# The rows of h without gaps, at another address, in a two-layer decoder trunk on one core

## The chip, the core and the metric

The kernel runs on one NeuronCore of a Trainium2 chip. Its engines are PE (TensorE, matmuls; its weight loads are listed as PEld), DVE (VectorE), ACT (ScalarE), POOL (GpSimd) and SP (SyncE, which here issues DMAs). The core's memory SBUF has 128 partitions; a tile takes the same bytes in each of them, so "address" below means the byte within a partition. The metric is the device time in microseconds of one execution. Three runs of the kernel before took 2653.11, 2655.77 and 2656.17 us, median 2655.77.

## The reference

Two layers over 256 tokens of width 2048, all in float32. Layer 0 mixes tokens by an eight-head retention, layer 1 by a short gated convolution; each is followed by a SwiGLU feed-forward with an inner width of 5632. Every sub-layer does

```python
mod = (c_act @ w_mod[i] + b_mod[i])[:, None, :]
sh1, sc1, g1, sh2, sc2, g2 = jnp.split(mod, 6, axis=-1)
h = (rms_norm(x, norm1_g[i]) * (1.0 + sc1) + sh1).astype(x.dtype)
y = retention_mixer(h, ...)            # or short_conv_mixer
x = (x + g1 * y).astype(x.dtype)
h = (rms_norm(x, norm2_g[i]) * (1.0 + sc2) + sh2).astype(x.dtype)
x = (x + g2 * swiglu(h, ffn_w_in[i], ffn_w_out[i])).astype(x.dtype)
```

and a final RMSNorm closes the trunk. Nearly all the arithmetic is products of h, or of a result of such a product, with weight matrices that are read once from HBM.

## The kernel before

Activations stand transposed: 128 features on the partitions, the 256 tokens along the row. A matrix of 2048 features is 16 such row tiles. Each float32 value is split into two parts that a matmul takes at its fast float32 format, hi (the rounded value) and lo (what is left); an activation row holds 256 hi columns and then 256 lo columns. A weight block of 128x128 is split alike: raw weights come by DMA (`fetch`, L289, three buffers), ACT casts half of a raw tile to hi (L310) and DVE subtracts for lo (L313), two halves ahead of their use (`AHEAD`).

The order on PE is written out by the program; weights lie in HBM in exactly that order (`in_use_order`), so `take` (L318) hands out the blocks one after another. A product of activations with weights takes one of these forms:

- `product` (L345): for each row k and each column block, a **pair**: one matmul of hi against the row's 512 columns (L355) and one of lo against its 256 hi columns (L358). It is the form of both feed-forward inputs and of the convolution's input, which read h, and of all output projections, which read `mid` (feed-forward and convolution) or `rm` (retention).
- `packed` (L365): three matmuls of 256 columns (L378 to L380). It reads h in the retention's input, and mid or rm in the last block of an output.
- `values` (L794): h is the weight side and 512 columns of hi or lo stream past it (L801 to L803).
- `normed` (L470): the first column blocks of a feed-forward or convolution input, before the norm of x is known. `scaled_only` (L461) writes rows that lack the norm, `ends` (L479, L480) writes two more columns behind each half row with the shift, and three matmuls of 258 columns run on each row (L493 to L495). Meanwhile `modulated` (L453) makes the finished rows with the norm in them, in the same memory, for the column blocks that follow.

All engines but PE are ordered by a scheduling layer, which places an instruction as soon as what it reads is written and what it overwrites has been read.

h is one tile of 16 rows, `[P, KT, 2, S + 2]` floats, so a row takes 2 x 258 x 4 = 2064 bytes, of which the four columns of `ends` are a gap for the finished rows. In the built program the tile begins at byte 118496, which is 1760 modulo 2048; row j thus begins at 1760 + 16j modulo 2048. The tiles of mid and rm are 2048 bytes each and follow each other without a gap; all begin at 2016 modulo 2048. Weight tiles hi and lo begin at 1760 modulo 2048.

The input of the first feed-forward has 44 column blocks in its first part, of which `normed` takes 6, and 44 in its second; the convolution's has 48, of which `normed` takes 6. With 16 rows each this makes stretches of 608, 704, 672, 608 and 704 pairs on h (3296 in all), with the outputs' stretches on mid between them.

Of the kernel before, what the change touches and what calls it, by code (L numbers as in the profile page):

```python
# [10 lines left out]
F32 = mybir.dt.float32  # L11
F32R = mybir.dt.float32r
I32 = mybir.dt.int32
AF = mybir.ActivationFunctionType
ALU = mybir.AluOpType
PSUM = bass.MemoryType.PSUM

P = 128
D = 2048
S = 256  # L20
KT = D // P
# [27 lines left out]
STEPS = (8, 8, 24, 12)  # L49
RAW_BUFS = 3  # L50
PART_BUFS = 4

Q0, K0, V0, G0 = 0, HEADS * DK, 2 * HEADS * DK, 2 * HEADS * DK + HEADS * DV
SH1, SC1, GT1, SH2, SC2, GT2 = range(6)
# [131 lines left out]
def trunk(ctx: ExitStack, tc: tile.TileContext, x_in, c_in, pos_in, w_mod, cols_in, tab_in, w_all, out):  # L186
    nc = tc.nc
    const = ctx.enter_context(tc.tile_pool(name="const", bufs=1))
    work = ctx.enter_context(tc.tile_pool(name="work", bufs=2))
    wpool = ctx.enter_context(tc.tile_pool(name="wpool", bufs=PART_BUFS))  # L190
    ps = ctx.enter_context(tc.tile_pool(name="ps", bufs=8, space=PSUM))
# [7 lines left out]
    def tmp(tag, shape=(P, S), dtype=F32, pool=work, bufs=None):  # L199
        return pool.tile(list(shape), dtype, tag=tag, name=name(tag), bufs=bufs)  # L200
# [8 lines left out]
    x = [t[:, j, :] for t in x4 for j in range(4)]  # L209
# [57 lines left out]
    def paced(n):  # L267

        units[0] += n
        due = 0  # L270
        for (a, i), (b, j) in zip(plan_mod, plan_mod[1:]):
            if units[0] >= a:
                due = min(j, i + (units[0] - a) * (j - i) // (b - a))
        allowed[0] = min(allowed[0] + n * MOST, 2.0) if n <= 64 else 0.0
        while todo and n_mod - len(todo) < due and allowed[0] >= 1.0:
            allowed[0] -= 1.0
            modulation(*todo.pop())

    def needed(layer, which, last=KT - 1):
        while any(m[:2] == (layer, which) and m[2] <= last for m in todo):  # L280
            modulation(*todo.pop())
# [36 lines left out]
    def take(group, k, col):  # L318

        assert order.pop() == (group, k, col)  # L320
        i = taken_cols[0] % HALF
        if i == 0:
            if ready and taken_cols[0]:
                ready.pop(0)
            while len(ready) < 1 + AHEAD * (units[0] >= first):
                n = len(ready)
                prepare()
                if len(ready) == n:
                    break
        taken_cols[0] += group.width  # L330
        return [t[:, i : i + group.width] for t in ready[0]]

    def bank():
        return ps.tile([P, 2, S], F32, tag="bank", name=name("bank"))
# [73 lines left out]
    def norm_sums(accs):  # L408

        pt = bank()  # L410
        for i, acc in enumerate(accs):
            for t in range(2):
                nc.tensor.matmul(
                    pt[:, 0, t : t + 1], acc[:, t * P : (t + 1) * P], ones[:, 0:1],
                    start=i + t == 0, stop=i == len(accs) - 1, skip_group_check=True,
                )
        return pt

    def norm_roots(pt, n):

        r = tmp("rs", (P, 2), bufs=4)
        nc.vector.tensor_scalar(r, pt[:, 0, 0:2], 1.0 / n, EPS, op0=ALU.mult, op1=ALU.add)
        r2 = tmp("rs", (P, 2), bufs=4)
        nc.gpsimd.tensor_tensor(r2, r, half, op=ALU.pow)
        return r2

    def norm_spread(r):

        pb = bank()
        for t in range(2):  # L430
            nc.tensor.matmul(
                pb[:, 0, t * P : (t + 1) * P], r[:, t : t + 1].to_broadcast([P, P]), ident, start=True, stop=True
            )
        return pb[:, 0, :]
# [18 lines left out]
    def modulated(h, j, rb, layer, norm):  # L453
        shifted(h, scaled(j, rb, layer, norm), j, layer, norm)

    hpool = ctx.enter_context(tc.tile_pool(name="hpool", bufs=1))

    h_all = hpool.tile([P, KT, 2, S + 2], F32R, tag="h", name="h")
    h = [h_all[:, j, :, :S] for j in range(KT)]

    def scaled_only(layer, norm, j):  # L461

        needed(layer, SC2 if norm else SC1, j)
        a = mod_a[layer][norm][:, j : j + 1]
        nc.scalar.activation(h[j][:, 0, :], x[j], AF.Identity, scale=a)
        nc.vector.scalar_tensor_tensor(
            h[j][:, 1, :], x[j], a, h[j][:, 0, :].bitcast(F32), op0=ALU.mult, op1=ALU.subtract
        )

    def normed(accs, layer, norm, g):  # L470

        needed(layer, SH2 if norm else SH1)
        shift = mod_s[layer][norm].unsqueeze(2).to_broadcast([P, KT, 2])
        ends = [h_all[:, :, i, S:] for i in range(2)]
        nc.scalar.copy(ends[0], shift)  # L479
        nc.vector.tensor_tensor(ends[1], shift, ends[0].bitcast(F32), op=ALU.subtract)  # L480
        banks = [bank().rearrange("p a b -> p (a b)")[:, : S + 2] for _ in g.cols]
        made = [0]

        def more(n):
            while made[0] < n:
                modulated(h[made[0]], made[0], root, layer, norm)
                made[0] += 1

        for k in g.ks:
            rows = [h_all[:, k, i, :] for i in range(2)]  # L490
            for c, pt in zip(g.cols, banks):
                hi, lo = take(g, k, c)
                nc.tensor.matmul(pt, hi, rows[0], start=k == 0, stop=False)  # L493
                nc.tensor.matmul(pt, hi, rows[1], start=False, stop=False)  # L494
                nc.tensor.matmul(pt, lo, rows[0], start=False, stop=k == KT - 1)  # L495
            if k == ROOTS_AT:
                r = norm_roots(norm_sums(accs), D)
            elif k == SPREAD_AT:
                root = tmp("rb", bufs=1)
                nc.scalar.copy(root, norm_spread(r))  # L500
            elif k > SPREAD_AT:
                more(min(k, made[0] + 2))
        more(KT)
        paced(len(g.cols) * len(g.ks))

        def total(pt, dst=None):
            end = tmp("end", (P, 1), bufs=2)
            nc.scalar.copy(end, pt[:, S : S + 1])
            t = tmp("low", bufs=3)
            nc.vector.tensor_tensor(t, pt[:, :S], root, op=ALU.mult)  # L510
            dst = tmp("sum", bufs=4) if dst is None else dst
            nc.scalar.activation(dst, t, AF.Identity, bias=end)
            return dst

        return [lambda dst=None, pt=pt: total(pt, dst) for pt in banks]
# [27 lines left out]
    with ExitStack() as inner:  # L543
# [353 lines left out]
        def ret_out(part, last):  # L897
            after = (lambda j: scaled_only(0, 1, j)) if last else None
            acc = output(RET_OUT[part], mid, (0, GT1), last, after, base=0)
            assert not asides  # L900
            for n in range(len(mid)):
                if ("mid", n) in tag_of:
                    free.append(tag_of.pop(("mid", n)))
            return acc
# [13 lines left out]
    def swiglu(layer, acc, after):  # L918
        n = FT // 2
        for part, groups in enumerate(FFN_IN):  # L920
            mid = [mpool.tile([P, 2, S], F32R, tag=f"mid{i}", name=name("mid")) for i in range(n)]
            pending, done = [], 0
            for i, g in enumerate(groups):
                pending += [sums(g)] if part or i else normed(acc, layer, 1, g)
                while len(pending) >= 2:
                    a, b = pending[:2]
                    pending = pending[2:]
                    s = a()
                    g1 = tmp("silu", pool=mpool, bufs=2)
                    nc.scalar.activation(g1, s, AF.Silu)  # L930
                    s = b()
                    m = tmp("m", pool=mpool, bufs=2)
                    nc.vector.tensor_tensor(m, s, g1, op=ALU.mult)
                    split(mid[done], m)
                    done += 1
            acc = output(FFN_OUT[part], mid, (layer, GT2), part == 1, after if part else None)
        return acc

    acc = swiglu(0, acc, lambda j: scaled_only(1, 0, j))


    mid = [mpool.tile([P, 2, S], F32R, tag=f"mid{i}", name=name("mid")) for i in range(KT)]
    pending, done = [], 0
    for i, g in enumerate(CONV_IN):
        pending += [sums(g)] if i else normed(acc, 1, 0, g)
        while len(pending) >= 3:
            pb, pc, pu = pending[:3]
            pending = pending[3:]
            j = done
            b, c, u = pb(tmp("bsum", pool=mpool, bufs=2)), pc(), pu()  # L950
# [10 lines left out]
            split(mid[j], y)  # L961
            done += 1
    acc = output(CONV_OUT, mid, (1, GT1), True, lambda j: scaled_only(1, 1, j))

    parts = []
# [59 lines left out]
```

## Time and profile before

| | |
|---|---|
| median of three runs | 2655.77 us |
| the profiled execution's span, first to last instruction | 2658.0 us |
| TensorE clock granted, mean over the span | 0.996 |
| PE busy | 2622.0 us, 99% |
| DVE busy, ACT busy | 2019.7 us, 1260.0 us |
| mean DMA rate | 259 GB/s |
| retention with all its products | to 803 us |
| first feed-forward | 803 to 1543 us |
| convolution | 1543 to 1905 us |
| second feed-forward and final norm | 1905 to 2658 us |

A group's row on the page gives line, engine, operation, "written tile <- read tiles", the shapes and the number of instructions, then busy time and the mean ns of one, then the time for which its engine sat idle before them. Matmuls overlap each other, so the mean ns of one is longer than the distance between two starts. A row of the timeline begins with an instruction's start and duration in us. A row of the windows gives a stretch's length and, for each engine, its busy time and the number of its instructions, and then the granted clock, the busy share of the DMA engines and their rate.

### The profile page before, as it was taken

The numbers are of one execution on the slowest core, as the hardware profiler recorded it, in microseconds if no ns is written. First come the engines' busy times: TensorE is split into PE (matmuls) and PEld (weight loads), VectorE is DVE, ScalarE is ACT, GpSimd is POOL, SyncE is SP. The second block draws the span as 40 slices with busy tenths as digits, with TensorE's granted clock in tenths as the row PEclk, the third lists the DMA queues.
The fourth block names the chain that finished last, engine by engine and source line by source line (L and its number), as shares of the span: only waits on it lengthen the run. The fifth ranks groups of instructions, "written<-read, shape, count | busy, mean of one in ns | idle before, by whom it ended". The sixth has DMA issues, their size and how long they took to land.

```text
span 2658.0 us, 40105 instructions
## 1 busy us (share of the span) xinstructions
PE 2622.0 (99%) x16044; PEld 2340.2 (88%) x16044; DVE 2019.7 (76%) x2646; ACT 1260.0 (47%) x1819; POOL 153.5 (6%) x230
## 2 busy tenths in 40 slices
PE   7999999999999999999999999999999999999998
PEld 6998889889989888888888898888998888888887
DVE  7888988787698877777777889878887665555554
ACT  5545543444456444344444454444554443444443
POOL 0000000120000010100000001100000000000000
PEclk9999999999999999999999999999999999999999
DMA  9975668777676876777777758776776755444453
GB/s 397 396 274 220 224 232 315 263 269 280 239 271 252 319 282 262 300 269 280 283 278 276 273 219 321 289 276 258 265 269 256 264 220 190 184 187 189 190 190 127
DMA packets 96958, 687.70 MB, mean 259 GB/s; under 512 B 10753, under 2 KB 12545, under 8 KB 13825
## 3 DMA queue, kind: packets, MB, share of 16 engines
q1 hardware_dynamic: 96194, 684.48, 67.6%
q8 instruction: 125, 2.05, 0.3%
q10 hardware_dynamic: 576, 0.66, 0.1%
q14 instruction: 63, 0.52, 0.1%
HBM read 682.99 MB, written 2.10 MB: 258 GB/s over the span
## 4 chain that ended last, share of the span: by engine, by line
PE 75%; issue 19%; DVE 3%; DMA 1%; ACT 0%; POOL 0%; SPq 0%; POOLq 0%; ACTq 0%; DVEq 0%
PE bank L355 35%; PE bank L358 18%; PE bank L380 4%; PE bank L378 4%; PE bank L379 4%; PE bank L802 2%; PE bank L803 2%; PE bank L801 2%; PE bank L494 1%; PE bank L493 1%; PE bank L495 1%; DMA raw<-w_all 1%; DMA raw<-w_mod 1%; DVE lo L313 1%; DVE raw L619 0%
## 5 line engine op out<-in xcount | busy, mean ns | idle before, releaser
L313 DVE TENSOR_TENSOR lo<-raw,hi 128x1024 fp32r<-128x1024 f32 x912 | 1112.6, 1224 | 550.1 <-ACT hi L310 548.1
L310 ACT CAST hi<-raw 128x1024 fp32r<-128x1024 f32 x912 | 953.6, 1050 | 1101.8 <-PE bank L355 632.4
L355 PE MATMUL bank<-h,hi 128*128 128x512 f32 x3296 | 1155.2, 395 | 0.0
L358 PE MATMUL bank<-h,lo 128*128 128x256 f32 x3296 | 926.2, 281 | 0.0
L355 PEld LDWEIGHTS bank<-h,hi 128*128 128x128 f32 x3296 | 623.0, 189 | 144.1
L358 PEld LDWEIGHTS bank<-h,lo 128*128 128x128 f32 x3296 | 623.3, 189 | 0.0
L355 PE MATMUL bank<-mid,hi 128*128 128x512 f32 x1604 | 557.4, 394 | 0.0
L358 PE MATMUL bank<-mid,lo 128*128 128x256 f32 x1604 | 446.0, 278 | 0.0
L244 DVE SCALAR_TENSOR_TENSOR raw<-raw,cb 128x2048 f32<-128x2048 f32 x160 | 365.7, 2286 | 12.5 <-DMA raw<-w_mod 12.0
L355 PEld LDWEIGHTS bank<-mid,hi 128*128 128x128 f32 x1604 | 301.2, 188 | 70.2
L358 PEld LDWEIGHTS bank<-mid,lo 128*128 128x128 f32 x1604 | 301.5, 188 | 0.0
L380 PE MATMUL bank<-h,lo 128*128 128x256 f32 x1024 | 292.0, 285 | 6.2 <-DVE lo L313 6.2
L378 PE MATMUL bank<-h,hi 128*128 128x256 f32 x1024 | 291.9, 285 | 3.5 <-ACT h L644 3.5
L379 PE MATMUL bank<-h,hi 128*128 128x256 f32 x1024 | 291.3, 284 | 0.0
L380 PEld LDWEIGHTS bank<-h,lo 128*128 128x128 f32 x1024 | 195.7, 191 | 7.1 <-DVE lo L313 7.1
L378 PEld LDWEIGHTS bank<-h,hi 128*128 128x128 f32 x1024 | 197.3, 193 | 3.9 <-ACT h L644 3.8
L379 PEld LDWEIGHTS bank<-h,hi 128*128 128x128 f32 x1024 | 195.9, 191 | 0.2 <-DVE h L645 0.2
L355 PE MATMUL bank<-rm,hi 128*128 128x512 f32 x496 | 175.9, 399 | 0.1
L358 PE MATMUL bank<-rm,lo 128*128 128x256 f32 x496 | 139.5, 281 | 0.0
L355 PEld LDWEIGHTS bank<-rm,hi 128*128 128x128 f32 x496 | 93.3, 188 | 22.7 <-DVE rm L395 0.4
L802 PE MATMUL bank<-lo,h 128*128 128x512 f32 x256 | 101.8, 398 | 4.2 <-DVE lo L313 4.2
L801 PE MATMUL bank<-hi,h 128*128 128x512 f32 x256 | 102.2, 399 | 0.0
(155 smaller groups left out, 2190.2 us busy)
## 6 DMA issues: line engine op xcount, KB each, us to landing
raw<-w_all SPq DMA_DIRECT2D x456, 1024.0 KB, 4.9
raw<-w_mod SPq DMA_DIRECT2D x192, 1024.0 KB, 5.1
x<-x_in SPq DMA_DIRECT2D x4, 512.0 KB, 5.7
decay<-tab_in SPq DMA_DIRECT2D x8, 128.0 KB, 3.7
out<-out SPq DMA_DIRECT2D x4, 256.0 KB, 3.1
out<-out ACTq DMA_DIRECT2D x3, 128.0 KB, 2.7
out<-out SPq DMA_DIRECT2D x1, 384.0 KB, 2.6
out<-out ACTq DMA_DIRECT2D x1, 256.0 KB, 3.2
```

The costliest lines, as they stand in the source:

```text
L244: nc.vector.scalar_tensor_tensor(raw, raw, 1.0, cb, op0=ALU.mult, op1=ALU.mult, accum_out=total)
L310: nc.scalar.copy(hi, raw)
L313: nc.vector.tensor_tensor(lo, raw, hi.bitcast(F32), op=ALU.subtract)
L355: nc.tensor.matmul(pt, hi, h, start=fresh and k == g.ks[0], stop=False, skip_group_check=True)
L358: nc.tensor.matmul(pt[:, 1, :], lo, h[:, 0, :], start=False, stop=last and k == g.ks[-1], skip_group_check=True)
L378: nc.tensor.matmul(pt, hi, h[:, 0, :], start=first, stop=False, skip_group_check=True)
L379: nc.tensor.matmul(pt, hi, h[:, 1, :], start=False, stop=False, skip_group_check=True)
L380: nc.tensor.matmul(pt, lo, h[:, 0, :], start=False, stop=last, skip_group_check=True)
L493: nc.tensor.matmul(pt, hi, rows[0], start=k == 0, stop=False)
L801: nc.tensor.matmul(o, ht[:, 0, :], hi, start=k == 0, stop=False)
L802: nc.tensor.matmul(o, ht[:, 0, :], lo, start=False, stop=False)
L803: nc.tensor.matmul(o, ht[:, 1, :], hi, start=False, stop=k == KT - 1)
```

## The change

The finished rows of h and the rows that lack the norm get a layout each, in one flat tile. Finished row j is 512 floats at `ROW_AT + 512 j`: rows are 2048 bytes apart, hi and lo halves adjoin, and with `ROW_AT` = 64 floats they all begin at 2016 modulo 2048, as those of mid and rm do. (The tile now begins at byte 104160, again 1760 modulo 2048.) Rows that lack the norm, with the two columns of `ends`, keep the layout of 516 floats from the same start (`h_open`); so the columns of `ends` now share bytes with finished rows. The tile grows by 2048 bytes, and the scratch of dynamic DMAs shrinks from 16384 to 2048 bytes; all other tiles move down by a multiple of 2048 bytes (14336 for those that stand before h, 12288 for those behind it).

```diff
+ROW_AT = 64
+HROWS = KT * 2 * (S + 2) + 2 * S
+SCRATCH = 2048
...
-    h_all = hpool.tile([P, KT, 2, S + 2], F32R, tag="h", name="h")
-    h = [h_all[:, j, :, :S] for j in range(KT)]
+    ROW, OPEN = 2 * S, 2 * (S + 2)
+    h_all = hpool.tile([P, HROWS], F32R, tag="h", name="h")
+    h = [h_all[:, ROW_AT + ROW * j : ROW_AT + ROW * (j + 1)].rearrange("p (a b) -> p a b", a=2) for j in range(KT)]
+    h_open = h_all[:, ROW_AT : ROW_AT + KT * OPEN].rearrange("p (j a b) -> p j a b", j=KT, a=2)
...
-        nc.scalar.activation(h[j][:, 0, :], x[j], AF.Identity, scale=a)
+        row = h_open[:, j, :, :S]
+        nc.scalar.activation(row[:, 0, :], x[j], AF.Identity, scale=a)
         nc.vector.scalar_tensor_tensor(
-            h[j][:, 1, :], x[j], a, h[j][:, 0, :].bitcast(F32), op0=ALU.mult, op1=ALU.subtract
+            row[:, 1, :], x[j], a, row[:, 0, :].bitcast(F32), op0=ALU.mult, op1=ALU.subtract
         )
...
-        ends = [h_all[:, :, i, S:] for i in range(2)]
+        ends = [h_open[:, :, i, S:] for i in range(2)]
...
-            rows = [h_all[:, k, i, :] for i in range(2)]
+            rows = [h_open[:, k, i, :] for i in range(2)]
...
-    nc = bacc.Bacc("TRN2", target_bir_lowering=False, num_devices=1)
+    nc = bacc.Bacc("TRN2", target_bir_lowering=False, num_devices=1, dynamic_dma_scratch_size=SCRATCH)
```

No instruction is added or taken away, and PE, POOL and SP keep their order (line numbers of the changed kernel are 3 to 6 higher). On ACT and DVE one instruction each moves: the `ends` of the convolution's norm (L479 and L480, in the changed kernel L485 and L486). Before, ACT wrote them during the second part of the first feed-forward's input, between two casts of weights:

```order
L387 COPY low_13411<-bank_13320 128x256
L930 ACTIVATE silu_13415<-sum_13413 128x256
L310 CAST hi_13428<-raw_13426 128x1024
L479 CAST h<-s_86 128x16x2
L310 CAST hi_13448<-raw_13426 128x1024
L387 COPY low_13417<-bank_13368 128x256
```

Now that place reads on without it, and it stands 66 rows later, near the end of that part:

```order
L390 COPY low_14257<-bank_14203 128x256
L485 CAST h<-s_86 128x16x2
L313 CAST hi_14311<-raw_14309 128x1024
L397 CAST mid_11959<-m_14261 128x256
L313 CAST hi_14331<-raw_14309 128x1024
```

On DVE its partner moves with it, to a place between two instructions that finish a column block (`sum`, then `m`):

```order
L316 TENSOR_TENSOR lo_14290<-raw_14267,hi_14289 128x1024
L392 TENSOR_TENSOR sum_14259<-bank_14203,low_14257 128x256
L486 TENSOR_TENSOR h<-s_86,h 128x16x2
L939 TENSOR_TENSOR m_14261<-sum_14259,silu_14255 128x256
L316 TENSOR_TENSOR lo_14312<-raw_14309,hi_14311 128x1024
```

The write itself is the same; it has to come after the last reader of the finished rows whose bytes it now overwrites.

## The prediction

> **What bounds the kernel now.** I read the page first (busy shares, then the chain that ended last, then the costliest groups).
>
> ```profile
> PE 2622.0 (99%) x16044; PEld 2340.2 (88%) x16044; DVE 2019.7 (76%) x2646; ACT 1260.0 (47%) x1819; POOL 153.5 (6%) x230
> PE 75%; issue 19%; DVE 3%; DMA 1%; ACT 0%; POOL 0%; SPq 0%; POOLq 0%; ACTq 0%; DVEq 0%
> ...
> L355 PE MATMUL bank<-h,hi 128*128 128x512 f32 x3296 | 1155.2, 395 | 0.0
> L358 PE MATMUL bank<-h,lo 128*128 128x256 f32 x3296 | 926.2, 281 | 0.0
> L355 PE MATMUL bank<-mid,hi 128*128 128x512 f32 x1604 | 557.4, 394 | 0.0
> L358 PE MATMUL bank<-mid,lo 128*128 128x256 f32 x1604 | 446.0, 278 | 0.0
> L355 PE MATMUL bank<-rm,hi 128*128 128x512 f32 x496 | 175.9, 399 | 0.1
> L358 PE MATMUL bank<-rm,lo 128*128 128x256 f32 x496 | 139.5, 281 | 0.0
> ```
>
> PE is busy 99% of the span, and the products at L355/L358 wait for nothing (idle 0.0 or 0.1). So only what one pair (L355 plus L358) costs can move the end. The same pair of instructions has three prices: 395+281 on h, 394+278 on mid, 399+281 on rm. These durations overlap; what a pair costs is the distance between starts, so I cut the span into stretches of one kind and counted L355 in each:
>
> ```profile
> core 0: us, PE busy (x) PEld busy (x), PEclk, DMA share, GB/s
> 839.30:1052.30 213.00, 213.00 (x608) 114.85 (x609) 1.00 0.77 291
> 1052.30:1174.30 122.00, 122.00 (x353) 66.07 (x353) 1.00 0.72 275
> 1174.30:1421.00 246.70, 246.70 (x705) 133.06 (x705) 1.00 0.74 282
> 1847.00:1897.00 50.00, 50.00 (x143) 26.64 (x142) 1.00 0.81 306
> 380.00:440.00 60.00, 60.00 (x171) 31.93 (x170) 1.00 0.76 289
> ```
>
> A count takes in a matmul that straddles an edge, so it is one too high at times. Rows one and three are h: 213.0/608 = 350.3 ns and 246.7/704 = 350.4 ns a pair. Row two is mid: 122.0/352 = 346.6 ns. Row four is mid too, late in the conv output, and row five is rm: 60.0/170 = 353 ns, and row four about as much. PE is never idle, the granted clock is 1.00, DMA share and rate differ little: one instruction pair, three prices, 346.6, 350.4 and 353.
>
> **What sets the price.** In the built program mid and rm rows are 2048 bytes apart without a gap: all begin at one remainder modulo 2048 (2016). h rows are 2064 bytes apart, so row j begins 16j bytes further on, and its low half 8 bytes off the grid of its high half. But mid has both prices at one remainder. The timeline shows how it goes from one to the other in the conv output:
>
> ```profile
> 1841.90 0.39 PE L355 MATMUL bank<-mid,hi 128*128 128x512 f32 x1
> ...
> 1842.24 0.40 PE L355 MATMUL bank<-mid,hi 128*128 128x512 f32 x1
> ...
> 1842.59 0.40 PE L355 MATMUL bank<-mid,hi 128*128 128x512 f32 x1
> ...
> 1843.30 0.40 PE L355 MATMUL bank<-mid,hi 128*128 128x512 f32 x1
> ...
> 1843.65 0.40 PE L355 MATMUL bank<-mid,hi 128*128 128x512 f32 x1
> ...
> 1844.00 0.40 PE L355 MATMUL bank<-mid,hi 128*128 128x512 f32 x1
> ...
> 1844.36 0.40 PE L355 MATMUL bank<-mid,hi 128*128 128x512 f32 x1
> ```
>
> Up to 1842.59 two pairs take 0.69 us (a **fast cycle**, 346.6 a pair); from 1843.30 three take 0.35, 0.35 and 0.36, 1.06 together (a **slow cycle**, 353.3 a pair), and it stays so to the stage's end. What happened at 1842.59 is in the rows of the weight loads and of DVE:
>
> ```profile
> 1842.24 0.19 PEld L358 LDWEIGHTS bank<-mid,lo 128*128 128x128 f32 x1
> ...
> 1842.64 0.19 PEld L358 LDWEIGHTS bank<-mid,lo 128*128 128x128 f32 x1
> ```
> ```profile
> 1841.36 1.22 DVE L313 TENSOR_TENSOR lo<-raw,hi 128x1024 fp32r<-128x1024 f32 x1
> ```
>
> The load of lo begins with the L355 matmul before it (1842.24 both), but once 0.05 us after it (1842.64 against 1842.59), since DVE had finished that lo only at 1842.58. The matmul behind it was not late; the rhythm between loads and matmuls was, and it did not come back. So, on rows of one remainder, PE has two self-holding rhythms, and the start of a stretch decides which. On today's h rows I found no such choice: every stretch costs 350.4, since the remainder that moves on with k pulls it back each 16 rows.
>
> **The change, part by part.**
>
> *Five stretches of L355/L358 on h:* 608+704+672+608+704 = 3296 pairs. After the change their rows lie as mid's do, so the bounds are mid's own two prices: 346.6 gives -3.8 x 3296 = -12.5 us, 353.3 gives +2.9 x 3296 = +9.6 us. Which? Two run on from a mid stretch; three begin behind the three-matmul groups of L493 to L495. The nearest row for that is where a stretch on the 2016 remainder begins behind such groups, in the retention's output (L378 to L380 end at 349.87, then):
>
> ```profile
> 349.87 0.40 PE L355 MATMUL bank<-rm,hi 128*128 128x512 f32 x1
> ...
> 350.21 0.40 PE L355 MATMUL bank<-rm,hi 128*128 128x512 f32 x1
> ...
> 350.56 0.40 PE L355 MATMUL bank<-rm,hi 128*128 128x512 f32 x1
> ...
> 350.92 0.40 PE L355 MATMUL bank<-rm,hi 128*128 128x512 f32 x1
> ```
>
> After one pair it is in the slow cycle (0.35, then 0.36). The present entry on h looks alike:
>
> ```profile
> 839.25 0.39 PE L355 MATMUL bank<-h,hi 128*128 128x512 f32 x1
> ...
> 839.60 0.40 PE L355 MATMUL bank<-h,hi 128*128 128x512 f32 x1
> ...
> 839.96 0.40 PE L355 MATMUL bank<-h,hi 128*128 128x512 f32 x1
> ```
>
> The groups before it keep their layout (their rows still step by 16 bytes), so the entry should arrive in this phase again. I take the slow price, +9.6.
>
> *The stretches on mid that follow:* an h stretch runs into the next mid stretch without a break (PE 213.00 of 213.00, then 122.00 of 122.00), and mid would then have the same remainder as what came before. Now mid falls into the fast cycle straight after h. If h is slow, mid inherits it: (352+330) x 2 in the FFN outputs and some 79 pairs before 1842.59, 1443 pairs x 6.7 = +9.7 us; if it finds the fast cycle by itself, 0. I take +9.7, since neither cycle was left in any stretch without a late load or a break; the lower end 0 is a rival.
>
> *Three-matmul groups on h (L378 to L380, 1024 of them):* on the mid layout the trace has them too.
>
> ```profile
> L378 PE MATMUL bank<-h,hi 128*128 128x256 f32 x28 | 7.9, 282 | 0.0
> L380 PE MATMUL bank<-h,lo 128*128 128x256 f32 x27 | 7.6, 283 | 0.0
> L379 PE MATMUL bank<-h,hi 128*128 128x256 f32 x27 | 7.6, 282 | 0.0
> ```
> ```profile
> L378 PE MATMUL bank<-mid,hi 128*128 128x256 f32 x21 | 6.0, 283 | 0.0
> L380 PE MATMUL bank<-mid,lo 128*128 128x256 f32 x20 | 5.7, 284 | 0.0
> L379 PE MATMUL bank<-mid,hi 128*128 128x256 f32 x20 | 5.7, 283 | 0.0
> ```
>
> The first is h from 443 to 453 us, the second mid from 1536 to 1543: 1 ns more a matmul, x 3072 = +3.1 us; bounds 0 (the early groups partly wait for DVE) to +3.1. I take +3.
>
> *Values (L801 to L803):* 768 matmuls that load h as weights. In a clean stretch (590 to 610 us):
>
> ```profile
> L801 PE MATMUL bank<-hi,h 128*128 128x512 f32 x28 | 11.0, 394 | 0.0
> ```
>
> No row has such weights at the new remainder. A 512-column matmul lasts 394 to 399 in the rows above, and 390 at the shortest single one (839.25): 768 x (-4 to +5) = -3 to +4 us. I take +1.
>
> *The moved pair (L479, L480):* one 221 ns cast on ACT and its 191 ns partner on DVE, for the second layer's first norm, come some 66 ACT rows later, since the columns they write now lie in other rows' bytes. Three of each run in all:
>
> ```profile
> L479 ACT CAST h<-s x3: 204/221/222, 790.9 to 1901.2; 128x32 fp32r<-128x32 f32 x3
> ```
> ```profile
> L480 DVE TENSOR_TENSOR h<-s,h x3: 186/191/194, 796.5 to 1902.8; 128x32 fp32r<-128x32 f32 x3
> ```
>
> Behind them ACT waits with its hi cast and DVE with its lo; the loads run two halves ahead, so 0. Without that cover 0.4 us, and a late lo, which could change the cycle of that stretch. Writers of h change their addresses, not their sizes: 0. The smaller DMA scratch takes nothing away: the page's list of DMA issues has SP's and ACT's queues alone. 0.
>
> **Sum:** 9.6 + 9.7 + 3 + 1 = +23 us on the profile's span of 2658.0, so 2681. That span lies 2.2 us above the median of the three runs (2655.8; 2653.1 to 2656.2), so as a median 2679.
>
> **Rivals.**
>
> *A, fast throughout (the other side).* The h stretches enter the fast cycle and keep it: -12.5 + 3 + 1 = -8.5, 2647. For it: each mid stretch that begins straight after h rows entered the fast cycle within a pair or two, and no load is late in h stretches. Against it: the entry above. It decides at the first two pairs behind L495, three times alike.
>
> *B, h slow, mid fast.* Mid finds the fast cycle at its own start, or some stretches go one way and some the other: +9.6 + 3 + 1 = +13.6, 2669. Against it: nothing separates the stretches.
>
> *C, no effect.* The price follows from the sequence of instructions, not from addresses: 0, 2656. For it: mid shows two prices at one remainder. Against it: h costs 350.4 in every stretch. The Trainium skill ("TensorE: Matmul & The Clock Gate", Part 2, step 1) says PE has two independent SBUF read ports, so that loading the next weights takes no read bandwidth from the running matmul; and in "Back-to-back issue gap" it gives N/2.4 + 2.5 ns, in which no address appears. By those, this rival holds, at an estimated 325 ns a pair. The trace disagrees on both: 346.6 to 353 ns, and a load 0.05 us late changed the price of what followed.
>
> **Chances.** Slow throughout 0.42, A 0.30, B 0.18, C 0.10. From 0.2% (5.3 us) on a change can be told from none. Faster: A, with a little of B's mixtures, 0.32. Same: C, 0.10. Slower: 0.58. The likeliest gives 2679, its own range 2674 to 2684. A holds too much to be left out, so the range runs from 2645 (A's 2647 less part of what L801 may gain) to 2684 (L801 at its dear end).
>
> **What would show it.** Windows over the five h stretches: 353 ns a pair (704 pairs in 248.7 us) is the forecast, 346.6 (244.0) rival A, 350.4 (246.7) rival C. The mid stretch after each: 353 against 346.6 tells the forecast from B. The mean duration of L355 on h goes to 399 or to 394; L378 on h to 283. I am wrong if the pairs behind L495 run 0.35, 0.34 from the first, or if any stretch of h has a third price.

## The result: 0.7% slower

The changed kernel takes 2676.8 us (median of four runs, 2672.47 to 2678.85), the kernel before 2655.97 us (median of four, 2653.11 to 2656.6). The ratio is 1.0071, 95% interval 1.0059 to 1.0083: it is slower by 16 to 22 us. The forecast was 2679.

The page of the profiled execution after (its line of engines and the groups of L358; L358 and L361 are now the two matmuls of a pair):

```profile
PE 2636.9 (99%) x16044; PEld 2343.9 (88%) x16044; DVE 2019.6 (76%) x2646; ACT 1258.9 (47%) x1819; POOL 156.5 (6%) x230
...
L358 PE MATMUL bank<-h,hi 128*128 128x512 f32 x3296 | 1164.8, 399 | 0.0
...
L358 PE MATMUL bank<-mid,hi 128*128 128x512 f32 x1604 | 567.0, 399 | 0.0
...
L358 PE MATMUL bank<-rm,hi 128*128 128x512 f32 x496 | 173.4, 395 | 0.1
```

PE has the same 16044 matmuls and is busy 14.9 us longer (2622.0 before); DVE and ACT are as they were. A matmul of 512 columns (395 to 399 ns by the page) lasts longer than a pair takes, so the matmuls of one group overlap each other, and the group's busy time is the length of its stretches. It can be divided by the count: h 1164.8 us / 3296 = 353.4 ns a pair (before 1155.2, 350.5), mid 567.0 / 1604 = 353.5 (before 557.4, 347.5), and rm, which was not touched, 173.4 / 496 = 349.6 (before 175.9, 354.6).

The windows of after over stretches of h, mid, h, a late piece of the convolution's output, and h in the second feed-forward (L358 alone; busy time and count of PE, then of PEld, the granted clock, DMA share, GB/s):

```profile
836.80:1051.50 214.70, 214.70 (x609) 114.22 (x608) 1.00 0.77 289
1051.60:1175.80 124.20, 124.20 (x352) 66.05 (x352) 1.00 0.74 271
1176.00:1424.60 248.60, 248.60 (x705) 132.24 (x704) 1.00 0.75 279
1845.00:1895.00 50.00, 50.00 (x143) 26.64 (x142) 1.00 0.79 286
2288.50:2537.10 248.60, 248.60 (x705) 132.25 (x704) 1.00 0.52 186
```

Every one is 352 to 353 ns a pair: 214.7/608, 124.2/352, 248.6/704, 50.0/142, 248.6/704 (a count can be one off). The last moves 186 GB/s where the first moves 289, at the same price and at a granted clock of 1.00 in both; so it is neither DMA traffic nor the clock. The entry of the first stretch behind the three-matmul groups, by the timeline (start, duration):

```profile
836.27 0.39 PE L358 MATMUL bank<-h,hi 128*128 128x512 f32 x1
...
836.61 0.40 PE L358 MATMUL bank<-h,hi 128*128 128x512 f32 x1
...
836.98 0.40 PE L358 MATMUL bank<-h,hi 128*128 128x512 f32 x1
...
837.32 0.40 PE L358 MATMUL bank<-h,hi 128*128 128x512 f32 x1
...
837.67 0.40 PE L358 MATMUL bank<-h,hi 128*128 128x512 f32 x1
...
838.03 0.40 PE L358 MATMUL bank<-h,hi 128*128 128x512 f32 x1
```

After 0.34 and 0.37 it goes 0.34, 0.35, 0.36: three pairs take 1.05 to 1.06 us from the first on, the slow cycle of the prediction.

Two smaller things moved in the retention. From the timelines, of before and of after, the first and the last of a row of three-matmul groups on h (63 groups, 62 distances) and of a row of values (32 groups, 31 distances):

```profile
686.83 0.28 PE L378 MATMUL bank<-h,hi 128*128 128x256 f32 x1
...
708.97 0.28 PE L378 MATMUL bank<-h,hi 128*128 128x256 f32 x1
...
590.69 0.39 PE L801 MATMUL bank<-hi,h 128*128 128x512 f32 x1
...
612.27 0.39 PE L801 MATMUL bank<-hi,h 128*128 128x512 f32 x1
```
```profile
684.83 0.28 PE L381 MATMUL bank<-h,hi 128*128 128x256 f32 x1
...
707.15 0.28 PE L381 MATMUL bank<-h,hi 128*128 128x256 f32 x1
...
589.35 0.40 PE L807 MATMUL bank<-hi,h 128*128 128x512 f32 x1
...
610.46 0.39 PE L807 MATMUL bank<-hi,h 128*128 128x512 f32 x1
```

A group of three went from 357.1 to 360.0 ns (22.14/62, 22.32/62), three value matmuls from 696 to 681 (21.58/31, 21.11/31). That is 3 ns more for a group and 15 ns less for three value matmuls, where nothing waits. Some of them do wait for late weights, so the total is smaller: counted over all 1024 groups and 256 triples, from each start to the next start on PE and without PE's idle time, the two traces give +1.7 us and -3.2 us.

So the 16.1 us between the two spans (2658.0 and 2674.1) are, by this count, h +9.6, mid +9.6, three-matmul groups +1.7, values -3.2, rm -2.5, and +1.0 in which PE is idle between its first and its last matmul (25.2 us against 24.1); what is left is under 0.1.

### The profile page after: what moved, and what is told of

Read it like the earlier page. It is cut to its first block, busy times and chain, and to the rows that moved or that the text cites. A ratio compares the mean times of both kernels' runs of the same rounds, so it can differ in the third digit from the quotient of the medians.

```text
span 2674.1 us, 40105 instructions
## 1 busy us (share of the span) xinstructions
PE 2636.9 (99%) x16044; PEld 2343.9 (88%) x16044; DVE 2019.6 (76%) x2646; ACT 1258.9 (47%) x1819; POOL 156.5 (6%) x230
## 4 chain that ended last, share of the span: by engine, by line
PE 73%; issue 20%; DVE 4%; DMA 2%; ACT 1%; POOL 1%; SPq 0%; POOLq 0%; ACTq 0%; DVEq 0%
PE bank L358 35%; PE bank L361 17%; PE bank L381 4%; PE bank L383 4%; PE bank L382 4%; PE bank L808 2%; PE bank L807 2%; PE bank L809 2%; PE bank L500 1%; DMA raw<-w_all 1%; PE bank L499 1%; PE bank L501 1%; DVE lo L316 1%; DMA raw<-w_mod 1%; DVE raw L247 1%
## 5 line engine op out<-in xcount | busy, mean ns | idle before, releaser
L358 PE MATMUL bank<-h,hi 128*128 128x512 f32 x3296 | 1164.8, 399 | 0.0
L361 PE MATMUL bank<-h,lo 128*128 128x256 f32 x3296 | 925.7, 281 | 0.0
L358 PEld LDWEIGHTS bank<-h,hi 128*128 128x128 f32 x3296 | 619.3, 188 | 154.6
L361 PEld LDWEIGHTS bank<-h,lo 128*128 128x128 f32 x3296 | 622.6, 189 | 0.0
L358 PE MATMUL bank<-mid,hi 128*128 128x512 f32 x1604 | 567.0, 399 | 0.0
L361 PE MATMUL bank<-mid,lo 128*128 128x256 f32 x1604 | 450.5, 281 | 0.0
L358 PEld LDWEIGHTS bank<-mid,hi 128*128 128x128 f32 x1604 | 301.4, 188 | 75.2
L361 PEld LDWEIGHTS bank<-mid,lo 128*128 128x128 f32 x1604 | 303.0, 189 | 0.0
L358 PE MATMUL bank<-rm,hi 128*128 128x512 f32 x496 | 173.4, 395 | 0.1
L361 PE MATMUL bank<-rm,lo 128*128 128x256 f32 x496 | 137.6, 278 | 0.0
L358 PEld LDWEIGHTS bank<-rm,hi 128*128 128x128 f32 x496 | 93.0, 188 | 21.7 <-DVE rm L398 0.5
```

The lines of the kernel that those rows point to most:

```text
L358: nc.tensor.matmul(pt, hi, h, start=fresh and k == g.ks[0], stop=False, skip_group_check=True)
L361: nc.tensor.matmul(pt[:, 1, :], lo, h[:, 0, :], start=False, stop=last and k == g.ks[-1], skip_group_check=True)
```

## The experiments

Two theories were set against each other first. Theory 1 is the prediction's: on rows of one remainder PE can run in either cycle, the phase in which a stretch is entered decides, and what runs on from it inherits. Theory 2: the new address alone makes 353.3, however the stretch is entered. They are told apart by a different entry at unchanged addresses.

### A matmul more at the entry: 64, 128 and 240 columns

Behind the last row of each `normed` group, before the finished rows are read, one more matmul runs on columns of its bank that nothing reads. Three are added in all; nothing else changes.

```diff
-        banks = [bank().rearrange("p a b -> p (a b)")[:, : S + 2] for _ in g.cols]
+        wide = [bank().rearrange("p a b -> p (a b)") for _ in g.cols]
+        banks = [t[:, : S + 2] for t in wide]
...
+        spare = wide[-1][:, S + 2 : S + 2 + 64]     # 128, 240
+        nc.tensor.matmul(spare, hi, rows[0][:, :64], start=False, stop=True, skip_group_check=True)
```

> The changed kernel with one extra matmul of 64 columns behind the last group of each of the three norms (hi of the last weight block against the last row, into columns of the bank that nothing reads). Theory 1 (a stretch keeps the cycle it enters with, and the entry behind the norm's groups sets it): every stretch behind an entry that lands in the fast cycle costs 346.7 ns a pair instead of 353.3, h and mid alike, since nothing breaks them; if all three entries do, (608+352+704+330) x 2 + 672 + some 80 pairs x 6.7 ns = 32 us less, about 2645; an entry that lands in the slow cycle leaves its stretches at 353.3. Theory 2 (the price follows from the addresses of the rows and weights): 353.3 in all stretches, 2677. No other price of a pair than these two by either.

> As with 64 columns, with 128: another shift of the entry. Theory 1: each entry in the fast or in the slow cycle, three alike; 2645 or 2677 for the whole. Theory 2: 2677 and 353.3 as with every width.

> As with 64 columns, with 240: a third shift of the entry. Theory 1: 2645 or 2677, and over three widths and the reordered group at least one entry of each kind is likely (the trace of before had as many entries in the one cycle as in the other). Theory 2: 2677.

Measured, one execution each beside one of before at 2660.54 us: 2640.66 us with 64 columns, 2675.08 with 128, 2640.24 with 240. The pages' group of h, for 64, 128 and 240 in this order:

```profile
L358 PE MATMUL bank<-h,hi 128*128 128x512 f32 x3296 | 1143.1, 391 | 0.0
```
```profile
L358 PE MATMUL bank<-h,hi 128*128 128x512 f32 x3296 | 1164.9, 399 | 0.0
```
```profile
L358 PE MATMUL bank<-h,hi 128*128 128x512 f32 x3296 | 1142.9, 394 | 0.0
```

346.8, 353.4 and 346.8 ns a pair, at the same addresses: the two prices and nothing between them. The stretches on mid went with those on h each time (556.3, 567.0 and 556.3 us for 1604). One matmul at each entry, whose result nothing reads, made the kernel some 35 us faster or left it as it was, depending on its width. Theory 2 falls.

The start times, which the traces hold to the nanosecond, show that the cheap price is that of two rhythms. With 240 columns the pairs start 350 and 343 ns apart in turn, as on mid before the change; with 64 columns, from the third pair on, every pair is 346 or 347 ns behind the last. The slow cycle goes 350, 361, 349. The prediction's two rhythms are thus three, with two prices; "the cheap cycle" below stands for either of the cheap ones.

### Nothing added: another order in the last row

In the last row of each `normed` group, lo runs ahead of the two hi matmuls, so the last matmul before the pairs is one of hi.

```diff
+                last = k == KT - 1
+                if last:
+                    nc.tensor.matmul(pt, lo, rows[0], start=False, stop=False)
                 nc.tensor.matmul(pt, hi, rows[0], start=k == 0, stop=False)
-                nc.tensor.matmul(pt, hi, rows[1], start=False, stop=False)
-                nc.tensor.matmul(pt, lo, rows[0], start=False, stop=k == KT - 1)
+                nc.tensor.matmul(pt, hi, rows[1], start=False, stop=last)
+                if not last:
+                    nc.tensor.matmul(pt, lo, rows[0], start=False, stop=False)
```

> The changed kernel, where the last row of each norm's groups takes its three matmuls in another order (lo against hi first, then hi against hi and against lo); no instruction is added. Theory 1: the entry behind it may land in the other cycle, three alike: 2645 or 2677. Theory 2: 2677.

Measured: 2640.63 us, before 2660.54. The timeline at the first entry, and the page's groups of h and mid:

```profile
833.59 0.40 PE L358 MATMUL bank<-h,hi 128*128 128x512 f32 x1
...
833.95 0.39 PE L358 MATMUL bank<-h,hi 128*128 128x512 f32 x1
...
834.30 0.39 PE L358 MATMUL bank<-h,hi 128*128 128x512 f32 x1
...
834.65 0.39 PE L358 MATMUL bank<-h,hi 128*128 128x512 f32 x1
...
834.99 0.39 PE L358 MATMUL bank<-h,hi 128*128 128x512 f32 x1
```
```profile
L358 PE MATMUL bank<-h,hi 128*128 128x512 f32 x3296 | 1142.9, 391 | 0.0
...
L358 PE MATMUL bank<-mid,hi 128*128 128x512 f32 x1604 | 556.3, 391 | 0.0
```

From the second pair on, two take 0.69 to 0.70 us (0.35, 0.35, 0.34: the even rhythm, 346 or 347 ns a pair), and 3296 pairs cost 1142.9 us, 346.8 each. The same instructions in the same memory, with three matmuls of 258 columns in another order at 18 places (six column blocks at each of three entries), are 36 us faster than the median of the changed kernel and 20 faster than the one execution of before beside it (over more executions, further down, it is 14.5). The price of a stretch of 600 pairs and more is settled in its first few.

### One entry alone

Only the convolution's entry, the second of three, gets that order (`turned` in place of `last` in the diff above).

```diff
+                turned = last and layer == 1 and not norm
```

> The changed kernel with the order of lo_first (lo ahead in the last row of the three-matmul groups) at the entry of the convolution alone, the second of three. Theory 1: each entry decides for itself, and what runs on from it inherits: 353.3 in the first feed-forward, 346.7 on the convolution's 672 pairs of h and its 240 of mid, 353.3 again in the second; (672+240) x 6.7 = 6.1 us less than the changed kernel, 2669 to 2671 us. Rival (the cycle is set once for the whole execution, or carried across the groups): all stretches behind the entry stay at 346.7, 19 us less, 2657; or none changes, 2676.

Measured: 2671.4 us. Windows over h and mid in the first feed-forward, h and mid in the convolution, and h in the second feed-forward (L358; columns as above without PEld):

```profile
837.09:1051.81 214.72, 214.72 (x608) 1.00 0.78 289
1425.04:1541.53 116.49, 116.49 (x330) 1.00 0.72 265
1585.58:1818.46 232.88, 232.88 (x672) 1.00 0.78 293
1818.56:1902.42 83.86, 83.15 (x240) 1.00 0.76 275
1944.28:2159.00 214.72, 214.72 (x608) 1.00 0.72 264
```

353.2, 353.0, then 346.5 (232.88/672) and 346.5 (83.15/240; one late weight holds L358 up for 0.7 us), then 353.2 again. Each entry decides for its own stretch and what runs on from it, and the three-matmul groups in between wipe it out. The span, 2669.6, is 4.5 us under that of the changed kernel; 6.1 were expected. The h stretch gave its 4.4 us and mid 1.6 by the pages (565.4 against 567.0); the wait took 0.7 back, and so did 1.1 us on rm (174.5 against 173.4), where the retention's second output ran in the dear cycle here and in the cheap one in the changed kernel.

### The gap, and an entry into it

The layout of before with the added matmul of 128 columns.

```diff
         h_all = hpool.tile([P, KT, 2, S + 2], F32R, tag="h", name="h")     # as before
...
+        nc.tensor.matmul(spare, hi, rows[0][:, :128], start=False, stop=True, skip_group_check=True)
```

> This is the layout of the kernel before (rows 2064 bytes apart), with one 128-column matmul added behind the last row of each three-matmul group on h. Theory 1 (rows at one remainder leave PE a choice of two cycles that the entry makes; rows that move on by 16 bytes pull it back and leave none): the h stretches keep 350.4 ns a pair whatever the entry, mid finds 346.6 by itself, and the time stays at that of before on the same chip, within 3 us. Rival (every layout has the two cycles, and the entry alone decides): h goes to 346.7 or to 353.3, and the time to -12 or +10 us and more.

Measured: 2660.15 us, before 2655.6 on the same chip.

```profile
L355 PE MATMUL bank<-h,hi 128*128 128x512 f32 x3296 | 1155.4, 395 | 0.0
...
L355 PE MATMUL bank<-mid,hi 128*128 128x512 f32 x1604 | 556.3, 393 | 0.0
```

h keeps its 350.5 ns (1155.4/3296, against 1155.2 before), and mid runs at 346.8 throughout. The time is 4.5 us above that of before on its chip, more than the 3 that were expected at most, but not on these stretches: its span, 2658.4, is that of the profiled execution of before (2658.0), in which the same groups take as long. On these rows this entry made no lasting difference, and the start times show why. A pair's distance depends on its row here: from 342 to 358 ns over the sixteen rows, and the same again, within 2 ns, in every column block. The first distances of the first stretch are 350, 360, 353 ns before and 402, 348, 347 with the added matmul; from the fourth pair on the two traces agree within 2 ns, but for some ten pairs behind a late weight at 924.5 us. It is one other entry, not a proof for all.

### The walk without the gap

The finished rows of the changed kernel are put 2064 bytes apart again, their halves still adjoining.

```diff
-    h = [h_all[:, ROW_AT + ROW * j : ROW_AT + ROW * (j + 1)].rearrange("p (a b) -> p a b", a=2) for j in range(KT)]
+    h = [h_all[:, ROW_AT + OPEN * j : ROW_AT + OPEN * j + ROW].rearrange("p (a b) -> p a b", a=2) for j in range(KT)]
```

> The changed kernel with its finished rows 2064 bytes apart, halves adjoining: the walk by 16 bytes a row is back, the gap of 8 bytes between the halves is not. Theory 1 (the walk takes away the choice): 350.4 ns a pair on h, mid at 346.6, the time of before within 4 us. Rival (the gap between the halves did it): the two cycles on h, 353.3 or 346.7, and 2677 or 2640 us.

Measured: 2659.28 us.

```profile
L358 PE MATMUL bank<-h,hi 128*128 128x512 f32 x3296 | 1160.7, 396 | 0.0
...
L358 PE MATMUL bank<-mid,hi 128*128 128x512 f32 x1604 | 556.3, 391 | 0.0
```

Neither theory's number: 352.2 ns a pair on h, a price that no other layout had, with mid back at 346.8. By the start times the distances repeat from row to row again, from 344 to 360 ns. So on these rows, behind this entry, the walk does away with the two cycles, and mid is no longer handed the slow one, as theory 1 said; but the gap of 8 bytes was worth something too, 352.2 with the halves adjoining against 350.5 with it.

### Other addresses for rows that do not walk

```diff
-ROW_AT = 64
+ROW_AT = 0      # rows begin at 1760 modulo 2048
+ROW_AT = 72     # in another kernel: at 0 modulo 2048
```

The rows that lack the norm begin at `ROW_AT` too, so the groups ahead of each entry move by the same bytes.

> The changed kernel with its finished rows 256 bytes further down: all begin at 1760 modulo 2048 and no longer at 2016, 2048 bytes apart as in the changed kernel. Theory 1 (what counts is that the rows do not move on; their remainder itself does not matter beyond that): h at 346.7 or 353.3, no third price; since the groups ahead of the stretches are the same, 353.3 and 2677 us. Rival (the class 2016 itself matters, as that of mid and rm): a third price on h, and mid, whose rows stay at 2016, falls into 346.6 by itself as it does in the kernel before.

> The changed kernel with its finished rows 32 bytes further up: all begin at 0 modulo 2048, so at 0 and not at 32 modulo 64. Theory 1: the two cycles again, 346.7 or 353.3, and mid goes on in the one that it is handed, 2640 or 2677 us. Rival (the remainder modulo 64 sets the price): a price of its own on h, as the rows that walk by 16 bytes have one with 350.4, and mid at 2016 finds 346.6 by itself.

Measured: 2674.05 us at 1760, 2638.98 at 0, before 2655.6. Groups of h and mid, at 1760 and then at 0:

```profile
L358 PE MATMUL bank<-h,hi 128*128 128x512 f32 x3296 | 1164.8, 399 | 0.0
...
L358 PE MATMUL bank<-mid,hi 128*128 128x512 f32 x1604 | 567.0, 399 | 0.0
```
```profile
L358 PE MATMUL bank<-h,hi 128*128 128x512 f32 x3296 | 1142.8, 390 | 0.0
...
L358 PE MATMUL bank<-mid,hi 128*128 128x512 f32 x1604 | 556.3, 391 | 0.0
```

At 1760 h and mid are as at 2016, to the tenth of a us. The class 2016, shared with mid and rm, has no merit of its own; 1760 and 2016 lie 256 bytes apart, so they agree modulo 64, 128 and 256. At 0 the pairs are in the cheap cycle behind the plain entry, in the even rhythm of 346 or 347 ns, and two other groups changed. The same timelines as above, for the rows at 0:

```profile
679.72 0.28 PE L381 MATMUL bank<-h,hi 128*128 128x256 f32 x1
...
701.42 0.28 PE L381 MATMUL bank<-h,hi 128*128 128x256 f32 x1
...
584.17 0.40 PE L807 MATMUL bank<-hi,h 128*128 128x512 f32 x1
...
605.87 0.40 PE L807 MATMUL bank<-hi,h 128*128 128x512 f32 x1
```

21.70/62 = 350.0 ns for three matmuls of 256 columns (360.0 at 2016) and 21.70/31 = 700.0 for three value matmuls (681 at 2016). So theory 1 as it was put for these runs, that only the walk counts and not the remainder, holds between 1760 and 2016 and falls at 0: 32 bytes up make one form of product 2.8% cheaper and another 2.8% dearer.

The Trainium skill ("TensorE: Matmul & The Clock Gate", "Back-to-back issue gap") gives N/2.4 + 2.5 ns for what it calls the isolated gap of a matmul of N columns at full clock, an estimate of 327 ns for three of 256, and says in Part 2, step 1, that loading weights takes no read bandwidth from the running matmul. No row here comes down to that figure, and the 10 ns between the two addresses, for the same loads and matmuls without a wait, are in neither sentence.

### Is there a choice at 0?

The rows at 0 with the added matmul of 128 columns that left everything slow at 2016.

```diff
-ROW_AT = 64
+ROW_AT = 72
...
+        nc.tensor.matmul(spare, hi, rows[0][:, :128], start=False, stop=True, skip_group_check=True)
```

> The rows at 0 modulo 2048, with the added matmul of 128 columns that left all stretches at 353.3 with the rows at 2016. Theory 3 (rows at 0 modulo 64 leave PE the cheap cycle alone, as rows that walk leave it a mixed one): 346.7 on h and on mid again, 2639 us. Theory 1 (both cycles are open at 0 too, and it was the entry that came out otherwise): with this other entry it may be 353.3 throughout, 2675 us; 346.7 alone would not refute it.

Measured: 2638.25 us.

```profile
L358 PE MATMUL bank<-h,hi 128*128 128x512 f32 x3296 | 1143.0, 390 | 0.0
...
L358 PE MATMUL bank<-mid,hi 128*128 128x512 f32 x1604 | 556.3, 391 | 0.0
```

The cheap cycle again, behind the two entries (plain and 128 columns) that both give the slow one at 2016. In the timed execution of at_0 that was profiled, PE once waited 0.8 us in the middle of the first h stretch and took up the cheap cycle again (346.7 ns before and behind it). All fifteen stretches on h in the three runs at 0 go into the even rhythm within a few pairs, and go back to it behind every break. That speaks for theory 3, that rows at 0 leave PE one rhythm alone; two entries and a few breaks don't prove it.

### The two fast versions, timed

> The kernel of lo_first again, timed beside the kernel before. If what one execution showed is what the kernel does every time (346.7 ns on all stretches of h and mid), the ratio to before is 0.994 within 0.002, near 2640 us. If the cycle of a stretch is a matter of luck in each execution, the times scatter between 2640 and 2677 us.

> The kernel of at_0 again, timed beside the kernel before and lo_first_timed. From its one execution: three-matmul groups on h at 350 ns a triple and not 360, values at 700 ns and not 680, pairs at 346.7; 1024 x 10 ns less and 256 x 20 ns more against lo_first is 5 us less, part of it lost where the early groups wait for DVE, so 2637 to 2640 us. Rival: the entry in the cheap cycle was luck of that execution, and the times scatter up to 2677 us.

| kernel | median of 5, us | lowest to highest | ratio to before, 95% interval |
|---|---|---|---|
| before (9 runs) | 2657.28 | 2655.39 to 2662.5 | 1 |
| order of the last row turned, rows at 2016 | 2642.78 | 2639.86 to 2643.79 | 0.9941 (0.9928 to 0.9953) |
| rows at 0, order unchanged | 2639.53 | 2638.97 to 2645.13 | 0.9939 (0.9925 to 0.9953) |

Both beat both kernels, in every run; no run came near 2677, so the cycle isn't luck of an execution. The intervals don't tell the two apart. Small stretches do switch from one execution to another: of the two profiled executions of the turned order, the convolution's output ended in the cheap cycle in one and in the slow one in the other, and the retention's second output (180 pairs) the other way round. Each is about 1 us (1604 pairs on mid 556.3 and 557.3 us; 496 on rm 174.5 and 173.4), and between these two they cancel. They can be a part of the spread of 4 to 6 us; what makes the rest was not looked for.

## Why the prediction was right

**The h pairs.** +9.6 was the term, 1164.8 - 1155.2 = +9.6 the measurement; all five stretches took the slow cycle, from the first two pairs behind the three-matmul groups. That the entry decides, where the address leaves a choice, was an argument from one late weight load at 1842.64; the runs with another entry show it at 2016.

**Why slow, and not rival A.** The step was that the groups ahead keep their layout, so the entry arrives in the phase that went slow on rm. The result agrees, but the step was weaker than it looked, and that this entry came out slow is in part luck: of the five entries tried at 2016 (plain, 64, 128 and 240 columns, turned order) two went slow and three cheap, and with the rows at 0 groups in the same order led to the cheap cycle. Rival A was one such edit away. The turned order is A made true, and its span is 19.1 us under that of before (2638.9 against 2658.0) where A had -8.5. By the count from start to start, h gives -12.3 of it, values -4.7, rm -1.4, PE's idle time -1.4, mid -1.1 and the three-matmul groups +1.8: A had h right, and was off on the values (+1), the groups (+3) and on rm, mid and the idle time, which it left at nothing.

**Mid inherits.** Term +9.7, measured 567.0 - 557.4 = +9.6. In every run the stretches on mid began as h went, slow behind slow, cheap behind cheap, and cheap behind the walking rows; only the convolution's output changed over on its way at times. Rival B is refuted.

**Three-matmul groups.** The term was +3 out of 0 to +3.1; 3 ns more a group is what it said for groups that don't wait, but over all 1024 it came to +1.7. The rest are groups behind late weights or at the end of a row, 69 before and 63 now, and they cost no more than before.

**Values.** This is the term that was mis-sized: +1 was taken from bounds of -3 to +4, and -3.2 was measured, outside them. The step bounded it by single durations of 512-column matmuls (390 to 399 ns) on the assumption that the weight side's address shifts a matmul by no more than the moving side's does. The mean went to 389 in a clean stretch; what counts is the distance, 696 to 681 for three.

**Not in the sum: rm.** Its tiles keep their remainder and its instructions their order, so the prediction gave it no term, though its own rule said that a stretch is made by what comes before. It gives 2.5 us. The window 380 to 440 us, 171 pairs before, now has

```profile
380.00:440.00 60.00, 60.00 (x174) 32.46 (x174) 1.00 0.79 291
```

60/173 = 347 ns, the count being one too high, in place of 353. The entry behind the groups on h did not change over: it is as slow as the one that the prediction shows (0.35, 0.36, 0.35, 1.06 together). But that entry holds for twelve pairs only. Other products interrupt this output four times, and the last of them, four small matmuls (L431 at 373.62 before, L434 now), stands ahead of the 196 pairs that make up most of it:

```profile
353.11 0.40 PE L358 MATMUL bank<-rm,hi 128*128 128x512 f32 x1
...
353.46 0.40 PE L358 MATMUL bank<-rm,hi 128*128 128x512 f32 x1
...
353.82 0.40 PE L358 MATMUL bank<-rm,hi 128*128 128x512 f32 x1
...
354.17 0.40 PE L358 MATMUL bank<-rm,hi 128*128 128x512 f32 x1
```
```profile
376.84 0.60 PE L434 MATMUL bank<-tab,rs 128*128 128x128 f32 x4
377.20 0.48 PE L358 MATMUL bank<-rm,hi 128*128 128x512 f32 x1
```

By the start times its five pieces went slow, slow, cheap, cheap, slow before and slow, cheap, cheap, slow, cheap now. So the 353 ns of rm that the prediction read between 380 and 440 us belong to an entry behind the four small matmuls and not to the one that it took as its nearest row; that entry was slow all the same, and the step stands. How a change ahead of it came through the interruptions is open. Of the -2.5 us, 1.1 (173.4 against the 174.5 of other runs) is the second output's 180 pairs, which come out either way. The flip of the first came in all runs with h's rows 2048 bytes apart and in walk_only; it did not come in gap_kick.

**The rest at nothing.** The moved pair (L485 at 1425.56, L486 at 1426.91) and the writers of h cost nothing that shows: in the changed kernel PE is never idle between the first entry on h and 2662 us.

**The sum.** +23.3 was forecast and +16.1 came out on the spans. Values (4.2 too high), rm (2.5) and the three-matmul groups (1.3) make nearly all of the difference, less the 1.0 of idle time that no term had. The median rose by 20.8, and that 2679 lies so close to 2676.8 is luck: the span of before is 2.0 us above the median of its times and that of after 2.7 below, where the prediction took 2.2 off for the changed kernel as well. These 4.7 us hid most of the 7 by which the sum was too high.

**Rival C**, no effect, is refuted by the same windows: 353 and not 350.4. The late load at 1842.64, which the prediction set against it, shows a rhythm that was lost; that a load slows a running matmul is shown by no run here.

## What to carry to other kernels

Where matmuls follow each other without a wait and the same pair shows several prices, cut the span into stretches of one kind, divide length by count, and look at the first few pairs of each. In this kernel rows at one address remainder locked PE into a cheap or a dear rhythm, 2% apart, that lasted for hundreds of matmuls and passed to the next stretch, and the order of a few matmuls ahead, or 32 bytes in the address, chose. So try a layout at two remainders and with two entries before judging it: this one was slower by 0.7% as it stood, and faster by 0.6% with another entry or another remainder.

## What the runs showed of the hardware that was not expected

- Moving h's rows from 2016 to 0 modulo 2048 changed products in opposite directions: 350.0 against 360.0 ns for three matmuls of 256 columns on h, 700.0 against 681 for three of 512 with h as weights. Why is open. Only 1760, 2016 and 0 and the two walks were tried, so which power of two the remainder has to be taken by, 64, 128 or 256, is open too.
- The three prices of a pair became four: 346.7, 350.5 and 353.3, and 352.2 for walking rows with adjoining halves. On walking rows the price is a mean over sixteen rows, from 342 to 358 ns before; what a row's own remainder does to its distance was not tried.
- Three matmuls of 64 or of 240 columns whose results nothing reads, one at each entry, saved 34 to 35 us against three of 128 on the same chip (2640.66 and 2640.24 against 2675.08, one execution each).
